# Input products of a gated recurrence in 512- and 256-column matmuls, two operands in other slots, and eight modulation blocks moved to the output projection

## The chip, the core and the metric

The kernel runs on one core of a Trainium2 chip. The metric is the device time of one execution in microseconds (us); each version is run several times and the median is taken. The engines are called as the profile calls them: PE (TensorE) multiplies, PEld loads its weights, DVE (VectorE) and ACT (ScalarE) work elementwise, SP issues the DMAs.

## The reference

One layer of a hybrid block on 256 tokens of width 2048, in f32. Every projection below is a dense product.

```python
mod = silu(c) @ ada_w + ada_b                    # six vectors of 2048: sh1, sc1, g1, sh2, sc2, g2
h = rmsnorm(x, norm1_g) * (1 + sc1) + sh1
z = h @ w_in                                     # split into q, kc, vc, ks, vs, kw, vw, g_nsa, lx, ly, ga, gb
o_a = nsa_attention(q, kc, vc, ks, vs, kw, vw, g_nsa, ...)   # 16 heads, 4 groups: compressed, selected, window branch
u = causal_dwconv(lx, conv_w, conv_b)            # 4 taps
r = sigmoid(blocks(u) @ w_a + b_a)               # 16 blocks of 128 x 128
i = sigmoid(blocks(u) @ w_i + b_i)
log_a = 8 * r * log_sigmoid(lam)
# scan over the tokens: s[t] = exp(log_a) * s[t-1] + sqrt(-expm1(2 * log_a)) * i * u
o_b = gelu(ly) * s
merged = sigmoid(ga) * (o_a @ proj_a) + sigmoid(gb) * (o_b @ proj_b)
x = x + g1 * (merged @ w_out)
h = rmsnorm(x, norm2_g) * (1 + sc2) + sh2
gate, val = split(h @ ffn_up)                    # 2 x 6144
x = x + g2 * ((gelu(causal_dwconv(gate)) * val) @ ffn_down)
return rmsnorm(x, final_g)
```

## The kernel before

Every dense product is done in three parts so that it keeps f32 accuracy in a faster format: weights W and activations X are each split into a rounded part and a rest, and the kernel sums X_hi W_hi, X_lo W_hi and X_hi W_lo. An activation tile `h1[:, kt, :]` therefore has 512 columns: 256 tokens of hi and, behind them, the same 256 tokens of lo.

Weights come in pieces of 1 MB, 128 x 2048. `stage` (L97) issues the DMA on SP's queue into one of four `raw` buffers. `split` (L102) turns each half of it into a `hi` tile (copy on ACT, L107) and a `lo` tile (subtraction on DVE, L108), three buffers of each. A split is issued at a raised priority. A piece in feature layout holds two output tiles of 128 features for eight k tiles.

Two helpers multiply such a piece. `dense_pair1` (L172) puts both output tiles into one bank, 256 columns each, and issues three 256-column products per weight tile: hi with X_hi, hi with X_lo, lo with X_hi (L185, L187, L188). `dense_pair` (L114) gives each output tile a bank of its own and issues two products per weight tile: hi with all 512 columns and lo with 256 (L130). Its bank holds two halves that have still to be added, and its products are kept in the order in which they are written (`keep_in_program_order`). `dense_tok` (L192) is the form with tokens on the partitions, for the gates, `w_proj`, `w_out` and `w_down`; all its products are 512 columns wide.

The stages in order of time are these. First the norm, the modulation and the projections for keys, values and queries. Then the attention and the input products of the recurrence (287 to 476 us): eight products `pr` of 32 weight tiles each into `lx` (L714 to L720), between them the attention units (g, t) of `attention` (L632), each with four heads of scores, softmax, transposes and the product `oT` (L693, L697). Then the recurrence (476 to 585 us): four tiles `bt` of 512 channels, each with the causal convolution on DVE (L740, L743), the gate products `lru_r` and `lru_i` on PE (L745, L747), sigmoids, tanh, exp and sqrt on ACT (L751 to L757), three 1024-wide steps and four scans on DVE (L758 to L762), and two products of the gelu branch (L765) with gelu (L767), product with the scan (L768) and split into `oB` (L771, L772). Then the merge (585 to 893 us), the output projection with `w_out` (893 to 984 us) and the FFN.

The modulation vectors g1, sc2, sh2 and g2 are 64 blocks of 128 numbers. Each is one 1 MB piece, multiplied by a row and summed in one 2048-wide pass on DVE (L234), followed by an addition of one column (L235). `filler(n)` issues the next n of these blocks where it is called: two behind each product of the lx loop (L720), two behind the gelu products with pr 0 and 4 (L773), two or four behind each `w_proj` product (L797).

The order of the instructions on each engine is not written out by hand. A scheduler sets it from dependencies, priorities and the point at which pools free their buffers. It keeps the loads on SP's queue, the activations that share a table (`tbl`) and the products of `dense_pair` in the order of the code. Tiles with the same tag share one slot: C0 to C7 hold, one after the other, `kvc`, the gathered keys of the compression (`gath`), the softmax results `pT`, `lx` (C4 to C7) and `oB`. `cmpb` holds the compressed values `vcmp` and the compressed probabilities in C7, and the first head's `p` of each attention unit lies in C3.

## Time and profile before

| what | value |
|---|---|
| runs | 1793.19, 1794.15, 1797.32 us (median 1794.15) |
| profiled execution | 1793.77 us, its span 1792.0 us |
| mean granted clock of PE | 0.997 of full speed |
| PE busy | 1771.6 us, 99% of the span, 10262 products |
| DVE busy | 1350.5 us, 75% |
| ACT busy | 881.9 us, 49% |
| DMA | 429.50 MB, mean 240 GB/s |

The busy shares are means over stages, so the windows by stage are read next to them. Matmuls are pipelined: a 256-column product is shown 0.28 us long, although the next one starts 0.12 us behind it. What a product costs PE is therefore read from the distance of the starts. A value in square brackets behind a row is the idle time of the engine before it, and the work that ended this idle time.

### The profile page before, as it was taken

The numbers are of one execution on the slowest core, as the hardware profiler recorded it, in microseconds if no ns is written. First come the engines' busy times: TensorE is split into PE (matmuls) and PEld (weight loads), VectorE is DVE, ScalarE is ACT, GpSimd is POOL, SyncE is SP. The second block draws the span as 40 slices with busy tenths as digits, with TensorE's granted clock in tenths as the row PEclk, the third lists the DMA queues.
The fourth block names the chain that finished last, engine by engine and source line by source line (L and its number), as shares of the span: only waits on it lengthen the run. The fifth ranks groups of instructions, "written<-read, shape, count | busy, mean of one in ns | idle before, by whom it ended". The sixth has DMA issues, their size and how long they took to land.

```text
span 1792.0 us, 25746 instructions
## 1 busy us (share of the span) xinstructions
PE 1771.6 (99%) x10262; PEld 1545.9 (86%) x10262; DVE 1350.5 (75%) x1976; ACT 881.9 (49%) x1202; POOL 0.2 (0%) x4
## 2 busy tenths in 40 slices
PE   8999999999999999999999999999999999999997
PEld 7999898888999888888888998888888888888886
DVE  7998897998698766767765997888555677766555
ACT  5644464655578444444445644444433444444443
POOL 0000000000000000000000000000000000000000
PEclk9999999999999999999999999999999999999999
DMA  9999864665646867777775566777655555555552
GB/s 350 379 335 355 288 245 161 235 212 203 221 173 227 303 237 290 286 292 281 294 266 195 186 235 235 282 282 282 239 193 200 191 188 188 188 188 188 190 198 106
DMA packets 64200, 429.50 MB, mean 240 GB/s; under 512 B 7088, under 2 KB 7376, under 8 KB 15568
## 3 DMA queue, kind: packets, MB, share of 16 engines
q1 hardware_dynamic: 63792, 427.08, 66.2%
q8 instruction: 80, 1.31, 0.3%
q10 hardware_dynamic: 288, 0.79, 0.1%
q14 instruction: 40, 0.33, 0.1%
HBM read 425.72 MB, written 2.11 MB: 239 GB/s over the span
## 4 chain that ended last, share of the span: by engine, by line
PE 86%; DVE 6%; DMA 4%; issue 2%; ACT 2%; SPq 0%; DVEq 0%; ACTq 0%
PE P L130 26%; PE P L204 12%; PE P L205 12%; PE P L203 12%; PE P L187 3%; PE P L188 3%; PE P L185 3%; DMA raw<-ada_w 2%; DVE lo L108 2%; PE P L464 2%; PE P L466 2%; PE P L465 2%; PE P L149 1%; PE P L148 1%; PE P L150 1%
## 5 line engine op out<-in xcount | busy, mean ns | idle before, releaser
L107 ACT ACTIVATE hi<-raw 128x1024 fp32r<-128x1024 f32 x588 | 622.0, 1060 | 764.5 <-PE P L205 325.5
L108 DVE TENSOR_TENSOR lo<-raw,hi 128x1024 fp32r<-128x1024 f32 x588 | 717.1, 1222 | 370.5 <-ACT hi L107 369.7
L130 PE MATMUL P<-h,hi 128*128 128x512 f32 x1344 | 463.9, 394 | 0.0
L130 PE MATMUL P<-h,lo 128*128 128x256 f32 x1344 | 366.4, 278 | 0.0
L130 PEld LDWEIGHTS P<-h,hi 128*128 128x128 f32 x1344 | 249.1, 188 | 54.9
L130 PEld LDWEIGHTS P<-h,lo 128*128 128x128 f32 x1344 | 252.4, 188 | 4.2
L234 DVE SCALAR_TENSOR_TENSOR raw<-raw,crow 128x2048 f32<-128x2048 f32 x64 | 146.2, 2285 | 3.6 <-DMA raw<-ada_w 3.2
L188 PE MATMUL P<-h,lo 128*128 128x256 f32 x512 | 147.6, 289 | 0.8 <-DVE lo L108 0.8
L187 PE MATMUL P<-h,hi 128*128 128x256 f32 x512 | 146.7, 287 | 0.0
L185 PE MATMUL P<-h,hi 128*128 128x256 f32 x512 | 146.7, 287 | 0.0
L464 PE MATMUL P<-h,hi 128*128 128x256 f32 x384 | 107.9, 285 | 0.3 <-ACT hi L107 0.3
L465 PE MATMUL P<-h,hi 128*128 128x256 f32 x384 | 107.6, 284 | 0.0
L466 PE MATMUL P<-h,lo 128*128 128x256 f32 x384 | 102.2, 284 | 0.0
L188 PEld LDWEIGHTS P<-h,lo 128*128 128x128 f32 x512 | 97.8, 191 | 1.8 <-DVE lo L108 1.4
L187 PEld LDWEIGHTS P<-h,hi 128*128 128x128 f32 x512 | 97.9, 191 | 1.4 <-issue 1.2
L185 PEld LDWEIGHTS P<-h,hi 128*128 128x128 f32 x512 | 97.9, 191 | 1.0 <-issue 0.7
L204 PE MATMUL P<-lo,ua 128*128 128x512 f32 x240 | 93.5, 390 | 0.3 <-DVE lo L108 0.3
L205 PE MATMUL P<-hi,ua 128*128 128x512 f32 x240 | 93.4, 389 | 0.0
L203 PE MATMUL P<-hi,ua 128*128 128x512 f32 x240 | 83.6, 389 | 0.0
L204 PE MATMUL P<-lo,h 128*128 128x512 f32 x192 | 75.5, 393 | 0.0
L464 PEld LDWEIGHTS P<-h,hi 128*128 128x128 f32 x384 | 74.0, 193 | 1.1 <-ACT hi L107 0.5
L205 PE MATMUL P<-hi,h 128*128 128x512 f32 x192 | 74.9, 390 | 0.0
(281 smaller groups left out, 3131.6 us busy)
## 6 DMA issues: line engine op xcount, KB each, us to landing
raw<-ada_w SPq DMA_DIRECT2D x96, 1024.0 KB, 5.0
raw<-w_up SPq DMA_DIRECT2D x96, 1024.0 KB, 4.8
raw<-w_down SPq DMA_DIRECT2D x48, 1024.0 KB, 4.9
raw<-w_lru SPq DMA_DIRECT2D x32, 1024.0 KB, 4.9
raw<-w_proj SPq DMA_DIRECT2D x32, 1024.0 KB, 5.1
raw<-w_gates SPq DMA_DIRECT2D x24, 1024.0 KB, 6.5
raw<-w_out SPq DMA_DIRECT2D x16, 1024.0 KB, 4.9
raw<-w_kv SPq DMA_DIRECT2D x24, 512.0 KB, 6.7
```

The costliest lines, as they stand in the source:

```text
L107: A.activation(hi[:, :n], raw[:, lo_col:lo_col + n], AF.Copy)
L108: V.tensor_tensor(lo[:, :n], raw[:, lo_col:lo_col + n], hi[:, :n].bitcast(F32), op=ALU.subtract)
L130: PE.matmul(ps[f][:, 0:256] if w else ps[f], hl[w][:, k * 256 + f * 128:k * 256 + f * 128 + 128], r[:, 0:256] if w else r, start=(kt == 0 ...
L185: PE.matmul(o, hi[:, sl], r[:, 0:256], start=(kt == 0 and f == 0), stop=False, skip_group_check=True)
L187: PE.matmul(o, hi[:, sl], r[:, 256:512], start=False, stop=False, skip_group_check=True)
L188: PE.matmul(o, lo[:, sl], r[:, 0:256], start=False, stop=(kt == n - 1), skip_group_check=True)
L203: PE.matmul(ps[j], xh, hi[:, w], start=(kt == 0), stop=False, skip_group_check=True)
L204: PE.matmul(ps[j], xh, lo[:, w], start=False, stop=False, skip_group_check=True)
L205: PE.matmul(ps[j], xl, hi[:, w], start=False, stop=(kt == n - 1), skip_group_check=True)
L234: V.scalar_tensor_tensor(raw, raw, 1.0, row, op0=ALU.mult, op1=ALU.mult, accum_out=modc[:, c:c + 1])
L464: PE.matmul(o, hi[:, sl], h1[:, kt, 0:256], start=first and f % 2 == 0, stop=False, skip_group_check=True)
L465: PE.matmul(o, hi[:, sl], h1[:, kt, 256:512], start=False, stop=False, skip_group_check=True)
```

## The change

The eight input products of the recurrence go through `dense_pair` without the fixed order, so each weight tile has one 512- and one 256-column product. `add_halves` adds the two halves: per output tile ACT copies the second half out of the bank and DVE adds the first half. The gelu branch keeps `dense_pair1`. `cmpb` moves to C3, `gat` to C7 and `gath` to C2, C4, C5 and C6; the first head's `p` goes into the small slot "xp". The softmax's short steps on DVE (clamp, reciprocal, product with the gates) are done once for two heads, and two heads' transposes follow together. The lx loop issues one modulation block per product where it issued two; in the merge the blocks are spread over the pieces of a product; eight blocks go between the pieces of the first three quarters of `w_out`. The shift columns of `hp` are written behind that loop. `w2t` and `hs`, and the two `gp` tiles of a gate pair in the FFN, share one tile each.

```diff
-        def dense_pair(pieces, rhs):
+        def dense_pair(pieces, rhs, pinned=True):
...
-                    for w in (0, 0, 1, 0, 1, 0, 1, 1) + (0, 1) * 4 if ip + half == 0 else (0, 1) * 8:
+                    for w in (0, 0, 1, 0, 1, 0, 1, 1) + (0, 1) * 4 if pinned and ip + half == 0 else (0, 1) * 8:
...
-                        tc.keep_in_program_order(
-                            PE.matmul(ps[f][:, 0:256] if w else ps[f], hl[w][:, k * 256 + f * 128:k * 256 + f * 128 + 128],
...
+                        mm = PE.matmul(ps[f][:, 0:256] if w else ps[f],
+                                       hl[w][:, k * 256 + f * 128:k * 256 + f * 128 + 128], r[:, 0:256] if w else r,
+                                       start=(kt == 0 and not w), stop=(kt == n - 1 and w == 1), skip_group_check=True)
+                        if pinned:
+                            tc.keep_in_program_order(mm)
             return ps
+
+        def add_halves(dst, p):
+            A.activation(dst, p[:, 256:512], AF.Copy)
+            with tc.high_priority(200):
+                V.tensor_tensor(dst, p[:, 0:256], dst, op=ALU.add)
...
-        def dense_tok(pieces, lhs, late=None):
+        def dense_tok(pieces, lhs, late=None, fills=()):
...
+                if ip in fills:
+                    filler()
...
-        cmpb = big.tile([128, 1024], F32R, tag="C7", name="cmpb")
+        cmpb = big.tile([128, 1024], F32R, tag="C3", name="cmpb")
...
-                g = big.tile([128, 16, 4, NCMP], F32, tag="C6", name="gat")
+                g = big.tile([128, 16, 4, NCMP], F32, tag="C7", name="gat")
...
-                    q = big.tile([128, 8, 2, 60], F32R, tag="C%d" % (2 + 2 * a + n), name="gath")
+                    q = big.tile([128, 8, 2, 60], F32R, tag="C%d" % (2, 4, 5, 6)[2 * a + n], name="gath")
...
-                if hh == 0:
-                    p = big.tile([128, 512], F32, tag="C3", name="p")
-                else:
-                    p = tmp.tile([128, 512], F32, tag=("r", "iu", "tt")[hh - 1], bufs=1, name="p")
...
+                p = tmp.tile([128, 512], F32, tag=("xp", "r", "iu", "tt")[hh], bufs=1, name="p")
...
+                heads.append(p)
+                if hh % 2 == 0:
+                    continue
+                w = sm[:, 1, hh - 1:hh + 1]
+                V.tensor_scalar(w, w, 1e-30, None, op0=ALU.max)
+                V.reciprocal(w, w)
+                V.tensor_tensor(w, w, gates[:, hh - 1:hh + 1, 1:3], op=ALU.mult)
+                turn_heads(hh - 1)
+                turn_heads(hh)
...
         for pr in range(8):
-            pl = dense_pair1([w_lru[pr, k] for k in range(2)], h1r)
-            A.activation(lx[pr // 2][:, 2 * (pr % 2):2 * (pr % 2) + 2],
-                         pl.rearrange("p (f t) -> p f t", f=2), AF.Copy)
+            ps = dense_pair([w_lru[pr, k] for k in range(2)], h1r, False)
+            for f in range(2):
+                add_halves(lx[pr // 2][:, 2 * (pr % 2) + f], ps[f])
             if units:
                 attention(*units.pop(0))
-            filler(2)
+            filler()
...
-                    ps = dense_tok([w_gates[n - 1, s, k] for k in range(4)], h1r)
+                    ps = dense_tok([w_gates[n - 1, s, k] for k in range(4)], h1r, fills=(1, 3))
...
-                ps = dense_tok([w_proj[n, s, k] for k in range(4)], rhs)
+                ps = dense_tok([w_proj[n, s, k] for k in range(4)], rhs, fills=(1, 3))
...
-                filler(2 if n == 0 else 4)
...
-            ps = dense_tok([w_out[n, k] for k in range(4)], lambda kt: mg[kt // 2][:, kt % 2])
+            ps = dense_tok([w_out[n, k] for k in range(4)], lambda kt: mg[kt // 2][:, kt % 2],
+                           fills=(0, 1, 3) if n < 2 else (0, 2) if n == 2 else ())
```

The scheduler now orders several stretches in another way. The first place is PE's order at the end of the attention. In the rows before, the last product of the lx loop (P_5013) ends, then come the last gate products of tile 1 of the recurrence (`lru_i`), then the first product of the gelu branch (P_5196).

```order
L185 MATMUL P_5013<-h1_169,hi_5102 128x256
L187 MATMUL P_5013<-h1_169,hi_5102 128x256
L188 MATMUL P_5013<-h1_169,lo_5103 128x256
L747 MATMUL lru_i_5146<-lt_5139,raw_5143 128x256 x2
L747 MATMUL lru_i_5160<-lt_5139,raw_5143 128x256 x2
L185 MATMUL P_5196<-h1_169,hi_5199 128x256
L187 MATMUL P_5196<-h1_169,hi_5199 128x256
L188 MATMUL P_5196<-h1_169,lo_5200 128x256
L185 MATMUL P_5196<-h1_169,hi_5199 128x256
```

After the change the last gate products of tile 1 (lru_i_4831) stand inside the third product of the gelu branch (P_5174), and the gate products of tile 2 (lru_r_5123, lru_i_5124) right behind them; the last attention product oT_4315 stands within the second gelu product, 23 rows further up.

```order
L191 MATMUL P_5174<-h1_169,hi_5177 128x256
L193 MATMUL P_5174<-h1_169,hi_5177 128x256
L194 MATMUL P_5174<-h1_169,lo_5178 128x256
L191 MATMUL P_5174<-h1_169,hi_5177 128x256
L193 MATMUL P_5174<-h1_169,hi_5177 128x256
L765 MATMUL lru_i_4831<-lt_4810,raw_4814 128x256 x2
L763 MATMUL lru_r_5123<-lt_5119,raw_5121 128x256
L765 MATMUL lru_i_5124<-lt_5119,raw_5121 128x256
L763 MATMUL lru_r_5123<-lt_5119,raw_5121 128x256
L765 MATMUL lru_i_5124<-lt_5119,raw_5121 128x256
L194 MATMUL P_5174<-h1_169,lo_5178 128x256
L191 MATMUL P_5174<-h1_169,hi_5177 128x256
```

Two and a bit of the eight gelu products have moved ahead of the end of tile 1's gate products, and tile 2's have moved up to them.

The second place is ACT's order at the same point, the activations of tile 1 (`lt` tiles, L751 to L757 before, L769 to L775 after; an `ACT_TABLE_LOAD` stands where the next function lies in another table). Before, the tanh, exp and sqrt stand between the copies `hi` of three pieces:

```order
L107 ACTIVATE hi_5329<-raw_5327 128x1024
L755 ACTIVATE lt_5142<-lt_5140 128x512
L756 ACT_TABLE_LOAD
L756 ACTIVATE lt_5140<-lt_5140 128x1024
L757 ACT_TABLE_LOAD
L757 ACTIVATE lt_5142<-lt_5142 128x1024
L107 ACTIVATE hi_5357<-raw_5327 128x1024
L107 ACTIVATE hi_5387<-raw_5385 128x1024
L767 ACT_TABLE_LOAD
L767 ACTIVATE lt_5139<-P_5196 128x512
L107 ACTIVATE hi_5415<-raw_5385 128x1024
L107 ACTIVATE hi_5506<-raw_5504 128x1024
```

After the change, the exp and the sqrt, two gelus and the sigmoids of tile 2 stand in one run ahead of hi_5263. The copy before it, hi_5235, stands six rows above the first row shown; three sigmoids, a tanh and a table load are between.

```order
L774 ACTIVATE lt_4811<-lt_4811 128x1024
L775 ACT_TABLE_LOAD
L775 ACTIVATE lt_4813<-lt_4813 128x1024
L785 ACT_TABLE_LOAD
L785 ACTIVATE lt_4810<-P_4867 128x512
L785 ACTIVATE lt_4810<-P_4997 128x512
L769 ACT_TABLE_LOAD
L769 ACTIVATE lt_5119<-lru_r_5123,cols_113 128x256
L770 ACTIVATE lt_5120<-lru_i_5124,cols_113 128x256
L769 ACTIVATE lt_5119<-lru_r_5123,cols_113 128x256
L770 ACTIVATE lt_5120<-lru_i_5124,cols_113 128x256
L107 ACTIVATE hi_5263<-raw_5233 128x1024
```

From one copy to the next there were at most five instructions here, and now there are 16, four of them table loads.

The third place is DVE's order for the same tile: the three 1024-wide steps, the scans, and the gelu branch's first product (L758 to L768 before, L776 to L786 after).

```order
L758 TENSOR_TENSOR lt_5141<-lt_5141,lt_5139 128x1024
L108 TENSOR_TENSOR lo_5330<-raw_5327,hi_5329 128x1024
L759 SCALAR_TENSOR_TENSOR lt_5142<-lt_5140,lt_5142 128x1024
L108 TENSOR_TENSOR lo_5358<-raw_5327,hi_5357 128x1024
L760 TENSOR_TENSOR lt_5142<-lt_5142,lt_5141 128x1024
L108 TENSOR_TENSOR lo_5388<-raw_5385,hi_5387 128x1024
L762 SCALAR_TENSOR_TENSOR lt_5141<-lt_5140,lt_5142 128x256 x4
L108 TENSOR_TENSOR lo_5416<-raw_5385,hi_5415 128x1024
L768 TENSOR_TENSOR lt_5139<-lt_5139,lt_5141 128x512
L108 TENSOR_TENSOR lo_5507<-raw_5504,hi_5506 128x1024
L772 TENSOR_TENSOR oB_5315<-lt_5139,oB_5315 128x2x256
L108 TENSOR_TENSOR lo_5535<-raw_5504,hi_5534 128x1024
```

After the change:

```order
L776 TENSOR_TENSOR lt_4812<-lt_4812,lt_4810 128x1024
L777 SCALAR_TENSOR_TENSOR lt_4813<-lt_4811,lt_4813 128x1024
L778 TENSOR_TENSOR lt_4813<-lt_4813,lt_4812 128x1024
L771 TENSOR_SCALAR lt_5119<-lt_5119,lsm4_90 128x256 x2
L780 SCALAR_TENSOR_TENSOR lt_4812<-lt_4811,lt_4813 128x256 x4
L108 TENSOR_TENSOR lo_5264<-raw_5233,hi_5263 128x1024
L786 TENSOR_TENSOR lt_4810<-lt_4810,lt_4812 128x512
L771 TENSOR_SCALAR lt_5119<-lt_5119,lsm4_90 128x256
L786 TENSOR_TENSOR lt_4810<-lt_4810,lt_4812 128x512
L771 TENSOR_SCALAR lt_5119<-lt_5119,lsm4_90 128x256
L776 TENSOR_TENSOR lt_5120<-lt_5120,lt_5119 128x1024
L108 TENSOR_TENSOR lo_5300<-raw_5297,hi_5299 128x1024
```

Before, a `lo` stood between any two steps of the tile; now lo_5264 stands behind the whole run with the scans, and the first steps of tile 2 (L771, L776) are among those that follow.

## Rows read from the trace of the kernel before

**Rows 1.** Page part 1: busy us, share of the span, instructions.

```profile
PE 1771.6 (99%) x10262; PEld 1545.9 (86%) x10262; DVE 1350.5 (75%) x1976; ACT 881.9 (49%) x1202; POOL 0.2 (0%) x4
```

**Rows 2.** Windows by stage, all engines.

```profile
core 0: us, PE busy (x) PEld busy (x) DVE busy (x) ACT busy (x) POOL busy (x), PEclk, DMA share, GB/s
287.00:476.00 189.00, 188.50 (x1297) 159.59 (x1296) 164.33 (x445) 109.78 (x266) 0.00 (x0) 1.00 0.56 199
476.00:585.00 109.00, 108.18 (x854) 106.10 (x853) 92.72 (x133) 84.79 (x111) 0.00 (x0) 1.00 0.59 212
893.00:984.00 91.00, 91.00 (x418) 75.20 (x418) 56.11 (x70) 45.37 (x63) 0.00 (x0) 1.00 0.66 239
```

**Rows 3.** Timeline of PE, recurrence: start, length, engine, line, tiles; 35 rows between.

```profile
500.20 0.28 PE L185 MATMUL P<-h,hi 128*128 128x256 f32 x1
...
504.52 0.28 PE L185 MATMUL P<-h,hi 128*128 128x256 f32 x1
```

**Rows 4.** Timeline of PE, FFN, where pairs run; 33 rows between.

```profile
1200.46 0.39 PE L130 MATMUL P<-h,hi 128*128 128x512 f32 x1
...
1206.36 0.40 PE L130 MATMUL P<-h,hi 128*128 128x512 f32 x1
```

**Rows 5.** Timeline of PE, three holes between 287 and 585 us.

```profile
329.14 0.55 PE L689 MATMUL tp<-cols,p 128*128 128x128 f32 x3 [0.50 <-ACT pcT L661]
516.91 0.39 PE L188 MATMUL P<-h,lo 128*128 128x256 f32 x1 [0.17 <-DVE lo L108]
551.78 0.28 PE L187 MATMUL P<-h,hi 128*128 128x256 f32 x1
552.71 0.38 PE L188 MATMUL P<-h,lo 128*128 128x256 f32 x1 [0.65 <-DVE lo L108]
```

**Rows 6.** Timeline of ACT, start of the recurrence.

```profile
486.14 0.47 ACT L751 ACTIVATE lt<-lru_r,cols 128x256 f32<-128x256 f32 x1
486.49 0.48 ACT L752 ACTIVATE lt<-lru_i,cols 128x256 f32<-128x256 f32 x1
487.83 0.61 ACT L755 ACTIVATE lt<-lt 128x512 f32<-128x512 f32 x1
488.47 1.28 ACT L756 ACT_TABLE_LOAD   x1
489.76 1.06 ACT L756 ACTIVATE lt<-lt 128x1024 f32<-128x1024 f32 x1
492.12 1.06 ACT L757 ACTIVATE lt<-lt 128x1024 f32<-128x1024 f32 x1
493.09 1.99 ACT L107 ACTIVATE hi<-raw 128x1024 fp32r<-128x1024 f32 x2
496.39 0.60 ACT L767 ACTIVATE lt<-P 128x512 f32<-128x512 f32 x1
```

**Rows 7.** The chain that ended last: start, length, engine, tile.

```profile
465.44 1.73 PE lru_r L745 x8
```

**Rows 8.** Timeline of DVE, recurrence.

```profile
483.10 0.35 DVE L753 TENSOR_SCALAR lt<-lt,lsm 128x256 f32<-128x256 f32 x1
497.76 2.43 DVE L762 TENSOR_TENSOR_SCAN lt<-lt 128x256 f32<-128x256 f32 x4
500.11 1.20 DVE L108 TENSOR_TENSOR lo<-raw,hi 128x1024 fp32r<-128x1024 f32 x1
501.23 0.68 DVE L768 TENSOR_TENSOR lt<-lt 128x512 f32<-128x512 f32 x1
510.71 0.74 DVE L740 TENSOR_SCALAR lt<-lx,cols 128x256 f32<-128x256 f32 x2
514.46 1.26 DVE L743 SCALAR_TENSOR_TENSOR lt<-lx,cols,lt 128x253 f32<-128x253 f32 x3
531.55 2.29 DVE L234 SCALAR_TENSOR_TENSOR raw<-raw,crow 128x2048 f32<-128x2048 f32 x1 [0.15 <-DMA raw<-ada_w]
```

**Rows 9.** Page part 6: DMA issues, KB each, us from issue to landing.

```profile
raw<-w_out SPq DMA_DIRECT2D x16, 1024.0 KB, 4.9
```

More of the change, by code (lines that the diff above doesn't have):

```diff
@@ L413, in compress @@
                 return
-            hs = tmp.tile([128, 4, 64], F32, tag="xp", bufs=2, name="hs")
+            hs = wh[:, 1].rearrange("p (g n) -> p g n", g=4)
             V.memset(hs, 0.0)
@@ L664, in attention, with turn_heads @@
             nj = 2 * (t + 1)
+            sm = tmp.tile([128, 2, 4, 2], F32, tag="sm", bufs=2, name="sm")
+            heads = []
+            def turn_heads(hh):
+                p = heads[hh]
+                for b in range(2):
+                    pb = p[:, b * nk:b * nk + nk]
+                    V.tensor_scalar(pb, pb, sm[:, 1, hh, b:b + 1], None, op0=ALU.mult)
+                tp = psx.tile([128, 512], F32, tag="t", bufs=1, name="tp")
+                for j in range(nj):
+                    PE.transpose(tp[:, j * 128:j * 128 + 128], p[:, j * 128:j * 128 + 128], ident)
+                for n in range(t + 1):
+                    A.activation(pT[n][:, :, hh, :], tp[:, n * 256:n * 256 + 256].rearrange("p (j q) -> p j q", q=128),
+                                 AF.Copy)
             for hh in range(4):
@@ L684, in attention @@
-                for b in range(2):
-                    pb = p[:, b * nk:b * nk + nk]
-                    V.tensor_scalar(pb, pb, sm[:, 4 + b:5 + b], None, op0=ALU.mult)
-                tp = psx.tile([128, 512], F32, tag="t", bufs=1, name="tp")
-                for j in range(nj):
-                    PE.transpose(tp[:, j * 128:j * 128 + 128], p[:, j * 128:j * 128 + 128], ident)
-                for n in range(t + 1):
-                    A.activation(pT[n][:, :, hh, :], tp[:, n * 256:n * 256 + 256].rearrange("p (j q) -> p j q", q=128),
-                                 AF.Copy)
+                p = tmp.tile([128, 512], F32, tag=("xp", "r", "iu", "tt")[hh], bufs=1, name="p")
@@ L822, in block_kernel @@
         sdev = small["sdev"]
-        for n in range(8):
-            sh = modc[:, 48 + 2 * n:50 + 2 * n].unsqueeze(2).to_broadcast([128, 2, 2])
-            A.activation(hp[n][:, :, 0, 256:258], sh, AF.Copy)
-            V.tensor_tensor(hp[n][:, :, 1, 256:258], sh, hp[n][:, :, 0, 256:258].bitcast(F32), op=ALU.subtract)
         def add_rows(ps, j, n, row):
@@ L855, in block_kernel @@
                 tc.keep_in_program_order(A.activation(warm, col("eps"), AF.Sqrt))
+        for n in range(8):
+            sh = modc[:, 48 + 2 * n:50 + 2 * n].unsqueeze(2).to_broadcast([128, 2, 2])
+            A.activation(hp[n][:, :, 0, 256:258], sh, AF.Copy)
+            V.tensor_tensor(hp[n][:, :, 1, 256:258], sh, hp[n][:, :, 0, 256:258].bitcast(F32), op=ALU.subtract)
         rstd(sdev, sums)
-        dr = tmp.tile([128, 2, 128], F32, tag="xp", bufs=2, name="dr")
+        dr = tmp.tile([128, 2, 128], F32, tag="xp", bufs=1, name="dr")
         for j in range(2):
@@ L881, in block_kernel @@
                     b = half * 24 + gr * 2 + f
[L882 removed]
+                    gps = tmp.tile([128, 2, 256], F32, tag="xp", bufs=1, name="gp") if f == 0 else gps
+                    gp = gps[:, f]
                     take(gp, f)
```

20 lines of the change are left out of this document (7 added, 13 removed).

## The prediction, made before the changed kernel was run

> **What bounds the kernel now.** First the page's busy shares: PE is busy 99% of the span of 1792.0 us [rows 1]. Busy PE is not PE at its peak, so next the windows by stage, where the granted clock stands at its upper level, 2.4 GHz, throughout [rows 2], and then the distances between the starts of matmuls. The stage with the attention and the input products of the recurrence (287 to 476 us) has DVE busy 164.33 of 189 us and ACT 109.78; the recurrence itself (476 to 585 us) has ACT busy 84.79 and DVE 92.72 of 109 us; in the output projection (893 to 984 us) DVE has 56.11 of 91 us [rows 2]. In a quiet stretch of the recurrence the starts of 128x256 products stand at a fixed distance: 12 triples in 4.32 us, 0.360 us a triple, 0.120 us each [rows 3]. In the FFN the pair of one 512-column and one 256-column product is as regular: 17 pairs in 5.90 us, 0.347 us a pair [rows 4]. PE therefore issues without holes nearly everywhere. In 287 to 585 us I find three holes worth naming [rows 5]: 329.14 (a transpose waits 0.50 us for ACT's pcT), 516.91 and 552.71 (a product waits 0.17 and 0.65 us for DVE's lo). Between the starts 551.78 and 552.71 lie 0.93 us instead of 0.12, so 0.81 us are lost, 0.16 more than the row's idle time; the other two lose 0.66 and 0.33 by the same addition. So PE is the bound, the time can fall only through fewer or shorter issue slots or through these holes, and each new hole is lost for good.
>
> **The change, part by part.** The sum is made against the profiled execution, 1793.8 us, 0.4 below the median of three runs.
>
> *Columns.* Eight input products of 32 weight tiles each, 256 triples, become 256 pairs of the kind that the FFN runs: 256 x (0.360 - 0.347) = **-3.2 us**, to be had only where PE issues without holes. At the same 768 columns three products take 13 ns more than two. The Trainium skill, TensorE: Matmul & The Clock Gate, section Back-to-back issue gap, gives N/2.4 + 2.5 ns for a full-clock product: an estimate from it is 328 ns for the triple and 325 for the pair, a gain of 0.7 us in all. The rows on both forms in this very kernel say otherwise, and the rule returns below as a rival.
>
> *Evictions.* Per product two 256-wide copies on ACT and two adds on DVE replace one 512-wide copy. No row has this shape out of a product's bank; the bounds are nothing and the 512-wide rows, 0.60 us on ACT [rows 6] and 0.68 on DVE [rows 8]. Both engines have slack there [rows 2], and eight modulation blocks of 2.29 us [rows 8] leave DVE in that stage, while 48 short softmax instructions go too. I take 0 for this. The hole at 329 us hangs on an attention chain with more slack now: **-0.66** (bounds -0.66 to +1).
>
> *Where the attention ends.* This is the edit that I think decides. The order of PE shows that with half of the modulation blocks gone the scheduler packs the input products more densely and the attention units further apart. Before, the gate products of tile 1 of the recurrence stand directly ahead of the first gelu product; now two and a bit of the eight gelu products stand ahead of them, and those of tile 2 stand right behind. The recurrence is no longer spread out. On ACT, 16 instructions now stand between hi_5235 and hi_5263, four of them table loads; with the prices below that run takes 11.3 us. Before, the run with the table loads was five instructions long (tanh, load, exp, load, sqrt) and took 5.3 us, from 487.83 to 493.09, and the three hi buffers covered it without a hole [rows 6]. On DVE lo_5264 now stands behind the scan of tile 1, where before a lo stood between any two steps.
>
> *First hole.* Count from the end of the last attention product oT_4315. ACT, by the lengths in [rows 6] less the 0.1 by which neighbours other than loads overlap there (sigmoids start 0.35 apart): oA 0.5, taken like a gelu of the same 512 columns; load 1.28; three sigmoids 1.08; tanh 0.53; sigmoid 0.36; hi_5235 1.0; three sigmoids 1.08; tanh 0.53; load 1.28; exp 1.07; load 1.28; sqrt 0.97; load 1.28; two gelus 1.0; load 1.28; three sigmoids 1.08: 15.6 us. Then DVE [rows 8]: two short multiplies 0.5, four scans 2.35, lo_5264 1.2: 4.1. So lo_5264 is there after 19.7 us. PE in the same time has 94 products at 0.120 and 12 gate matmuls; each of these stands twice in the trace, and eight records take 1.73 us [rows 7], so 0.43 each; 16.4 us. PE therefore waits 3.3 us with no time for the hand-overs between engines; with an estimated 0.5 us for five of them, **+3.8**. Bounds: 0, if the lead of the buffers is larger than the order lets me see, and 4.3. Behind lo_5264 on DVE stand the end of tile 1 and every later lo; behind PE's product the rest of the gelu branch.
>
> *After it.* PE has no lead left. From lo_5264 to lo_5786 the order gives PE 312 products and 8 gate products, 40.9 us. DVE has 13 splits at 1.13 (14.7), five other 1024-wide steps (5.7), two modulation blocks at 2.21 (4.4), four scans (2.35), eight 512-wide steps at 0.60 (4.8), 28 steps of the causal convolution at 0.39 and 0.33 (10.5) and six short multiplies at 0.27 (1.6): 44.1 us, each by its length in [rows 8] less the 0.08 by which neighbours overlap there. Without a single wait on DVE that is 3.3 us more than PE has; with its waits for the sqrt of tile 2 (ACT's loads again) and PE's for one late hi I come to 7.0. I take **+4.5**, nearer to the lower bound. The two holes of before in this stage go into this: **-1.1**.
>
> *Modulation blocks moved.* Eight blocks, each one 1 MB DMA on SP's queue, one 2048-wide pass on DVE and a short add, go into the first three quarters of the output projection: 8 x 2.3 = 18 us of DVE, which then has 74 of 91 us there. What they could hold up are the weight pieces behind them on SP, which wait for one of four raw buffers; a piece lands in 4.9 us [rows 9], PE needs 5.5 for its 24 products of 512 columns (0.23 each: the pair's 0.347 less 0.12) and at most one block stands between two pieces. In the merge before it the blocks are only spread between pieces. I count 0 (bounds 0 and +9: four of eight blocks each holding PE for their 2.3 us). The shift columns of hp written after that loop are short and in ACT's and DVE's order stand among the splits: 0.
>
> *Operand slots* change when tiles come free, not the work: 0; vcmp and the first p no longer sit where lx and the gathered keys go, which removes waits that no row shows.
>
> Sum: 1793.8 - 3.2 - 0.7 - 1.1 + 3.8 + 4.5 = **1797.1 us**, a slowdown of 0.18%.
>
> **The rivals.**
> *The recurrence keeps up.* Then only the first terms are left: 1793.8 - 3.2 - 0.7 - 1.1 = 1788.8, faster. It decides if ACT and DVE need no more than PE's 16.4 us from oT_4315 to lo_5264, that is if 3.3 us of the chain fall away. For it: before, a run of 5.3 us was covered without a hole [rows 6]. Against: this one is twice as long, and three buffers hold 3 x 2.88 us of products (24 at 0.120 each).
> *First hole only.* DVE's surplus is absorbed because PE's hole lets DVE run ahead: 1793.8 - 5.0 + 3.8 = 1792.6, the same. For it: DVE in 476 to 585 us has 16 us idle [rows 2]. Against: that idle time lies in another place of the order.
> *The columns give nothing.* Products between f32 attention matmuls may not reach the FFN's distance: at a gain of 0.7 us the sum is 1799.6. That is what the rule of the skill would give; the traces so far show 0.360 and 0.347 and bear it out badly.
> *The output projection stalls too.* Its four raw buffers now carry seven pieces a quarter; at +5 to +9 the time is 1802 to 1806.
>
> **How the numbers follow.** No measurement of this kernel can tell less than about 0.2% (3.6 us) from no change. The forecast, 1794.5 to 1801 by its own bounds, gets 0.55, of which 0.33 lies above 1797.7 and 0.22 below; the recurrence that keeps up 0.17, of which 0.15 are beyond 0.2%; the first hole alone 0.14; columns without gain 0.04; the projection 0.10. Slower 0.33 + 0.04 + 0.08 = 0.45, same 0.22 + 0.14 + 0.02 + 0.02 = 0.40, faster 0.15. The range 1789 to 1803 leaves out a part of the fastest case and of the slowest.
>
> **What would show it.** Products in pairs at 0.347 us in the input products of the recurrence (L129); PE idle for about 4 us, released by DVE's lo, some 16 us after the last oT, with four table loads on ACT in that time; further holes of 0.3 to 1.5 us, same releaser, in the 40 us behind; no idle PE in the output projection, DVE near 80% there. If the lo rows of that place come before PE asks for them, the third step is wrong and the time falls to 1789.

## The result and the profile after

The changed kernel takes 1807.51 us (median of 4 runs, 1807.3 to 1808.79), the kernel before 1795.49 us in the same count. The recorded ratio is 1.0075 with a 95% interval of 1.0063 to 1.0088, a little above the quotient of these two medians (1.0067): slower, by about four times what was forecast, and above the stated range. The profiled execution took 1807.71 us, 13.9 more than that of before; its span is 1805.7 us.

The page's busy shares of the changed kernel, which answer to [rows 1]:

```profile
PE 1774.8 (98%) x10006; PEld 1536.5 (85%) x10006; DVE 1353.4 (75%) x1944; ACT 889.1 (49%) x1214; POOL 0.2 (0%) x4
```

PE has 256 products less, as the pairs want it, and is idle 31 us instead of 20. The windows by stage (columns as in [rows 2]; the first four rows are the attention with the input products, the recurrence, the merge and the output projection, the last three are short stretches behind holes):

```profile
288.00:503.00 215.00, 213.17 (x1245) 171.65 (x1245) 160.83 (x402) 124.02 (x288) 0.00 (x0) 0.99 0.47 164
503.00:597.00 94.00, 86.35 (x650) 83.35 (x649) 78.66 (x117) 76.48 (x100) 0.00 (x0) 0.98 0.51 184
597.00:907.50 310.50, 308.20 (x1371) 254.46 (x1371) 220.96 (x242) 132.38 (x145) 0.00 (x0) 1.00 0.78 288
907.50:998.00 90.50, 90.50 (x416) 74.86 (x415) 70.42 (x92) 45.56 (x66) 0.00 (x0) 1.00 0.80 306
...
331.80:335.30 3.50, 3.50 (x12) 3.01 (x13) 3.23 (x9) 2.78 (x4) 0.00 (x0) 0.53 0.72 281
523.50:526.30 2.80, 2.80 (x15) 2.80 (x15) 2.80 (x6) 2.59 (x4) 0.00 (x0) 0.50 0.77 234
599.90:603.00 3.10, 3.10 (x14) 2.56 (x15) 3.10 (x4) 1.41 (x3) 0.00 (x0) 1.00 0.88 330
```

Attention and recurrence together went from 298 to 309 us. The attention's last product starts at 501.7 us instead of 474.2, so its stage is 26 us longer, and the recurrence, squeezed, has 94 us instead of 109. The output projection keeps its time with DVE at 70.42 of 90.50 us. The timeline of PE shows the holes, and at 394 us two starts of 512-column products with seven more pairs between them:

```profile
330.20 0.66 PE L685 MATMUL tp<-cols,p 128*128 128x128 f32 x4 [1.09 <-ACT pcT L671]
331.23 0.49 PE L711 MATMUL oT<-pcT,cmpb 47*128 47x512 f32 x1 [0.37 <-DVE oA L720]
338.92 0.70 PE L692 MATMUL s<-kT,qT 128*128 128x256 f32 x2 [0.37 <-ACT p L700]
...
394.27 0.39 PE L129 MATMUL P<-h,hi 128*128 128x512 f32 x1
...
397.05 0.40 PE L129 MATMUL P<-h,hi 128*128 128x512 f32 x1
...
520.59 0.38 PE L191 MATMUL P<-h,hi 128*128 128x256 f32 x1 [2.14 <-ACT hi L107]
523.13 0.58 PE L194 MATMUL P<-h,lo 128*128 128x256 f32 x1 [2.04 <-DVE lo L108]
557.24 0.39 PE L194 MATMUL P<-h,lo 128*128 128x256 f32 x1 [0.88 <-DVE lo L108]
567.73 0.38 PE L191 MATMUL P<-h,hi 128*128 128x256 f32 x1 [1.60 <-ACT hi L107]
599.88 0.50 PE L211 MATMUL P<-lo,oA 128*128 128x512 f32 x1 [2.30 <-DVE lo L108]
```

From the one start of 394.27 us to the other at 397.05 eight pairs take 2.78 us, 0.347 each, as in [rows 4]. The two holes at 518 to 523 us are the forecast first hole, which comes in two parts: PE waits for hi_5263 and, a few products on, for lo_5264. By the distance of the starts they lose 2.30 and 2.20 us. Later holes of 0.34 to 1.04 us wait for `lo`, as forecast; the largest, 1.76 us ahead of 567.73, waits for a copy `hi` on ACT. What stood on ACT meanwhile, of its timeline the two copies, the four loads and the sqrt of tile 1:

```profile
506.35 1.04 ACT L107 ACTIVATE hi<-raw 128x1024 fp32r<-128x1024 f32 x1
...
509.60 1.28 ACT L774 ACT_TABLE_LOAD   x1
511.96 1.28 ACT L775 ACT_TABLE_LOAD   x1
513.25 1.06 ACT L775 ACTIVATE lt<-lt 128x1024 f32<-128x1024 f32 x1
514.33 1.28 ACT L785 ACT_TABLE_LOAD   x1
516.73 1.28 ACT L769 ACT_TABLE_LOAD   x1
519.47 1.07 ACT L107 ACTIVATE hi<-raw 128x1024 fp32r<-128x1024 f32 x1
```

Between the two copies lie the 16 instructions with four table loads, from 507.3 to 519.5 us, 12.2 us; the forecast had 11.3 us for them (11.2 by its own prices). And DVE's timeline, at the same place and at the start of the merge:

```profile
514.34 1.23 DVE L777 SCALAR_TENSOR_TENSOR lt<-lt 128x1024 f32<-128x1024 f32 x1 [4.29 <-ACT lt L775]
519.53 2.43 DVE L780 TENSOR_TENSOR_SCAN lt<-lt 128x256 f32<-128x256 f32 x4
521.88 1.20 DVE L108 TENSOR_TENSOR lo<-raw,hi 128x1024 fp32r<-128x1024 f32 x1
...
593.46 2.43 DVE L780 TENSOR_TENSOR_SCAN lt<-lt 128x256 f32<-128x256 f32 x4
595.81 2.27 DVE L243 SCALAR_TENSOR_TENSOR raw<-raw,crow 128x2048 f32<-128x2048 f32 x1
598.60 1.22 DVE L108 TENSOR_TENSOR lo<-raw,hi 128x1024 fp32r<-128x1024 f32 x1
```

lo_5264 ends 20.8 us after ACT took up the last attention product (502.28 us); the forecast had 19.7. PE's own work in that time is about 16.5 us (from 502.1 to 523.1 us, less 4.5 of holes); the forecast had 16.4. At 595.81 a modulation block of the merge stands between the last scans and the first split that the merge waits for: the idle time of 2.30 us at 599.88, which the forecast did not have.

Where the input products stand against the attention is read from PE's timeline: the last of their 512 products starts at 471.60 us, 30 us ahead of the last attention product, and the row behind it, at 471.80, is of the gelu branch (L191).

```profile
471.60 0.36 PE L129 MATMUL P<-h,lo 128*128 128x256 f32 x1
```

### The profile page after: what moved, and what is told of

The parts are those of the page before. It is cut to its first block, busy times and chain, and to the rows that moved or that the text cites. A ratio compares the mean times of both kernels' runs of the same rounds, so it can differ in the third digit from the quotient of the medians.

```text
span 1805.7 us, 25201 instructions
## 1 busy us (share of the span) xinstructions
PE 1774.8 (98%) x10006; PEld 1536.5 (85%) x10006; DVE 1353.4 (75%) x1944; ACT 889.1 (49%) x1214; POOL 0.2 (0%) x4
## 4 chain that ended last, share of the span: by engine, by line
PE 91%; DVE 4%; ACT 3%; issue 1%; DMA 1%; DVEq 0%; SPq 0%; ACTq 0%
PE P L129 31%; PE P L211 12%; PE P L212 12%; PE P L210 12%; PE P L474 2%; PE P L475 2%; PE P L476 2%; PE P L155 1%; PE P L154 1%; DVE lo L108 1%; PE P L156 1%; PE P L468 1%; PE P L469 1%; PE P L467 1%; PE s L692 1%
## 5 line engine op out<-in xcount | busy, mean ns | idle before, releaser
L129 PE MATMUL P<-h,hi 128*128 128x512 f32 x1600 | 558.7, 396 | 0.0
L129 PEld LDWEIGHTS P<-h,hi 128*128 128x128 f32 x1600 | 297.9, 188 | 65.4 <-issue 0.7
L129 PEld LDWEIGHTS P<-h,lo 128*128 128x128 f32 x1600 | 301.4, 188 | 5.0 <-issue 0.7
L243 DVE SCALAR_TENSOR_TENSOR raw<-raw,crow 128x2048 f32<-128x2048 f32 x64 | 146.5, 2289 | 33.7 <-DMA raw<-ada_w 33.5
L474 PE MATMUL P<-h,hi 128*128 128x256 f32 x384 | 107.9, 285 | 0.0
L475 PE MATMUL P<-h,hi 128*128 128x256 f32 x384 | 107.8, 285 | 0.0
L191 PE MATMUL P<-h,hi 128*128 128x256 f32 x256 | 73.3, 287 | 3.7 <-ACT hi L107 3.7
L474 PEld LDWEIGHTS P<-h,hi 128*128 128x128 f32 x384 | 74.1, 193 | 0.3 <-issue 0.2
L475 PEld LDWEIGHTS P<-h,hi 128*128 128x128 f32 x384 | 74.2, 193 | 0.0
L193 PE MATMUL P<-h,hi 128*128 128x256 f32 x256 | 73.9, 289 | 0.0
L332 DVE SCALAR_TENSOR_TENSOR raw<-raw,crow 128x2048 f32<-128x2048 f32 x31 | 70.8, 2286 | 0.9 <-DMA raw<-ada_w 0.7
L476 PEld LDWEIGHTS P<-h,lo 128*128 128x128 f32 x384 | 70.6, 192 | 0.3 <-issue 0.2
```

The costliest lines, as they stand in the source:

```text
L129: mm = PE.matmul(ps[f][:, 0:256] if w else ps[f], hl[w][:, k * 256 + f * 128:k * 256 + f * 128 + 128], r[:, 0:256] if w else r, start=(kt ...
L193: PE.matmul(o, hi[:, sl], r[:, 256:512], start=False, stop=False, skip_group_check=True)
L243: V.scalar_tensor_tensor(raw, raw, 1.0, row, op0=ALU.mult, op1=ALU.mult, accum_out=modc[:, c:c + 1])
L474: PE.matmul(o, hi[:, sl], h1[:, kt, 0:256], start=first and f % 2 == 0, stop=False, skip_group_check=True)
L475: PE.matmul(o, hi[:, sl], h1[:, kt, 256:512], start=False, stop=False, skip_group_check=True)
L476: PE.matmul(o, lo[:, sl], h1[:, kt, 0:256], start=False, stop=last, skip_group_check=True)
```

## The experiments

Each run is compared with the kernel before on the same chip; the ratio has its 95% interval. "Hole" is time lost between two starts of products, beyond their usual distance; "half clock" is a stretch in which the profile shows a granted clock of 0.50. Holes and windows are those of one profiled execution each.

| run | what it is | median us | ratio to before |
|---|---|---|---|
| e1 | before, pairs alone | 1801.07 | 1.0035 [1.0023, 1.0048] |
| e2 | changed, compression's slots back | 1812.81 | 1.0100 [1.0086, 1.0114] |
| e3 | changed, merge's blocks back | 1809.47 | 1.0082 [1.0069, 1.0096] |
| e4 | changed, eight blocks back to the lx loop | 1808.44 | 1.0079 [1.0065, 1.0093] |
| e5 | changed, triples | 1800.77 | 1.0037 [1.0024, 1.0051] |
| e6 | changed, paced | 1802.24 | 1.0046 [1.0034, 1.0059] |
| e7 | before, pairs, paced | 1798.49 | 1.0031 [1.0018, 1.0043] |
| e8 | changed, softmax by head | 1804.28 | 1.0058 [1.0044, 1.0072] |
| e9 | before, pairs, paced more loosely | 1796.27 | 1.0012 [1.0003, 1.0021] |
| e10 | before, triples in two banks | 1793.85 | 0.9998 [0.9989, 1.0007] |
| e11 | before, operand slots alone | 1794.79 | 1.0001 [0.9992, 1.0011] |
| e12 | before, pairs, second piece paced | 1793.23 | 0.9998 [0.9989, 1.0007] |
| e13 | before, moved blocks alone | 1797.27 | 1.0021 [1.0012, 1.0030] |

**e1, the pairs alone.** Of the change only this, with its helpers:

```diff
-            pl = dense_pair1([w_lru[pr, k] for k in range(2)], h1r)
...
+            ps = dense_pair([w_lru[pr, k] for k in range(2)], h1r, False)
+            for f in range(2):
+                add_halves(lx[pr // 2][:, 2 * (pr % 2) + f], ps[f])
```

> The kernel before with the input products of the recurrence in 512- and 256-column products and nothing else changed. Theory A (the columns pay what the rows of before promise, and the recurrence is squeezed only where the columns meet the other operand slots): in its order of ACT no run between two copies hi is as long as the 16 instructions with four table loads of the changed kernel; the longest in the recurrence have 6 instructions with three loads, 6.3 us by the row lengths, so no hole over 1.5 us in the recurrence, and 1790 to 1793 us, 2 to 4 below before. Theory B (two banks for each product, out of four, are enough to squeeze the recurrence): holes of 2 us and more at the first gates, and at or above the time of before, 1796 to 1803 us.

It came as theory B has it in time and holes, 6.8 us above before; theory B's cause, the two banks, is tested in e10. PE's timeline:

```profile
471.23 0.66 PE L695 MATMUL tp<-cols,p 128*128 128x128 f32 x4 [0.72 <-ACT pcT L667]
472.64 0.66 PE L695 MATMUL tp<-cols,p 128*128 128x128 f32 x4 [0.75 <-ACT pT L697]
474.97 2.08 PE L751 MATMUL lru_r<-lt,raw 128*128 128x256 f32 x4 [1.68 <-ACT p L685]
478.45 1.09 PE L695 MATMUL tp<-cols,p 128*128 128x128 f32 x4 [0.68 <-DVE p L692]
525.22 0.38 PE L194 MATMUL P<-h,lo 128*128 128x256 f32 x1 [2.03 <-DVE lo L108]
```

In the last attention units PE has no products left to put between transposes and scores, and waits for the softmax itself: 5.8 us in 467 to 478 us. From the gates at 475 us to 483.8 us the granted clock stands at 0.50. The last input product starts 24 us ahead of the last attention product (466.5 and 491.0 us).

**e2, the slots.** `cmpb` back to C7, `gat` to C6, `gath` to C2 to C5.

```diff
-        cmpb = big.tile([128, 1024], F32R, tag="C3", name="cmpb")
+        cmpb = big.tile([128, 1024], F32R, tag="C7", name="cmpb")
...
```

> The changed kernel with cmpb, gat and gath in their slots of before (C7, C6, C2 to C5); wide products, paired softmax and the moved blocks stay. Theory A (the slots let the last two input products run ahead of the last attention units, and so squeeze the gates): the two holes of 2.3 and 2.2 us at 518 to 521 us, the half-clock stretch behind them and most of the later holes fall away, 8 to 10 us; 1797 to 1800 us. Theory B (slots only change when tiles come free): within 2 us of the changed kernel's 1807.5.

Neither: 5.3 us slower than the changed kernel by the medians, 4.5 by the ratios. `cmpb` lies in C7 until the attention ends, and the last quarter of lx wants C7. PE's timeline:

```profile
476.82 1.13 PE L763 MATMUL lru_r<-lt,raw 128*128 128x256 f32 x4 [1.70 <-ACT p L700]
482.61 0.58 PE L191 MATMUL P<-h,hi 128*128 128x256 f32 x1 [1.55 <-DVE lx L139]
531.80 0.58 PE L191 MATMUL P<-h,hi 128*128 128x256 f32 x1 [4.91 <-ACT hi L107]
```

A product waits for the lx eviction (L139), and the hole at the gates is 5.1 us instead of 4.5. With the pairs the new slots help; that the squeeze comes from them, theory A, is refuted.

**e3, the merge's blocks.** 

```diff
...
-                ps = dense_tok([w_proj[n, s, k] for k in range(4)], rhs, fills=(1, 3))
+                ps = dense_tok([w_proj[n, s, k] for k in range(4)], rhs)
...
                 m.append(sg)
+                filler(2 if n == 0 else 4)
```

> The changed kernel with the modulation blocks of the merge behind each product, as before; its order is the changed kernel's up to the merge. Theory A (the 2.5 us hole at 597 us is the modulation block that now stands between the last scans and the first splits of the merge): this hole goes and nothing else moves, 1804.5 to 1805.5 us. Theory B (DVE is late there from the recurrence anyway, the block only fills the wait): the hole stays at 1.5 us or more, 1807 us.

At the merge theory A holds: the block no longer stands ahead of the first split, and the hole falls from 2.47 to 0.49 us. But the time does not fall: the output projection takes 4.2 us more (95.0 instead of 90.9), 2.2 of them in holes that the changed kernel does not have (the first at 926.98) and most of the rest behind them, where the granted clock stands at 0.50 from 929.6 to 933.0 us. PE:

```profile
595.23 0.50 PE L211 MATMUL P<-lo,oA 128*128 128x512 f32 x1 [0.33 <-DVE lo L108]
...
926.98 0.73 PE L210 MATMUL P<-hi,mg 128*128 128x512 f32 x2 [0.68 <-ACT hi L107]
```

ACT, where the releaser is a weight piece that came late:

```profile
925.87 2.01 ACT L107 ACTIVATE hi<-raw 128x1024 fp32r<-128x1024 f32 x2 [4.13 <-DMA raw<-w_out]
```

**e4, the blocks of the lx loop.**

```diff
-            filler()
+            filler(2)
...
-                           fills=(0, 1, 3) if n < 2 else (0, 2) if n == 2 else ())
```

> The changed kernel with two modulation blocks per input product again and none in the output projection. Theory P, the prediction's own (the recurrence is squeezed because half of the blocks left the input products): the holes at 518 to 521 us go, 8 to 10 us less, 1798 to 1800 us. Theory A (columns and slots squeeze it, the blocks have no part): the same run of 16 instructions with four loads on ACT, the same two holes, and a time within 2 us of the changed kernel's 1807.5.

Theory A: the same two holes (2.54 and 2.20 us) and the same time. The prediction's own theory P had 1798 to 1800 us. The prediction's cause for the squeeze is refuted.

**e5, triples.** The reverse of e1's diff, on the changed kernel.

> The changed kernel with the input products of the recurrence as three 256-column products again, all else as changed. Theory A2, after the first four runs (with the pairs PE's order puts the input products ahead of the attention: an attention unit then takes about 25 us of PE's order instead of 20, the input products are used up two units before the end, and the last units and the first gates stand bare): with the triples the units are 20 us apart again, the first two holes and the half-clock stretch behind them go (6 us), later ones shrink by 2 or 3, the columns' 2 to 3 us are lost, the holes at 328 to 338 us and the one at the start of the merge stay: 1800 to 1803 us. Theory C (slots, softmax and blocks squeeze it by themselves): 1807 to 1810 us.

As theory A2 expects, 6.7 us below the changed kernel. The last attention product comes at 472.3 us instead of 501.7, and the holes of the recurrence sum to 1.6 us instead of 8.5.

**e6 and e7, paced.** One order edge on PE, on the changed kernel and on e1:

```diff
         for pr in range(8):
+            with ExitStack() as behind:
+                if pr:
+                    behind.enter_context(tc.issue_after(steps[pr].ins))
-            ps = dense_pair([w_lru[pr, k] for k in range(2)], h1r, False)
+                ps = dense_pair([w_lru[pr, k] for k in range(2)], h1r, False)
```

`steps[n]` is the last transpose of attention unit n.

> The changed kernel, same instructions, with one order edge on PE: input product n (n from 1) stands behind the last transpose of attention unit n, so that the products are not used up early. By its order the units are 19.5 us apart and the gates stand as before. Theory A2: the holes at 518 to 521 us, the half-clock stretch and most later ones go, 7 to 9 us; the holes at 328 to 338 us and at the merge stay: 1798 to 1801 us. Theory D (ACT and DVE have too much work for these stages in any order): holes of the same sum appear in the attention instead, where PE waits for a unit's transposes before it may go on with products: 1805 to 1810 us.

> The kernel before with the pairs for the input products and the same order edge, nothing else. Theory A2: the holes of the run with the columns alone at 467 to 480 us (6 us), its half-clock stretch (2 us) and the hole at 523 us (2 us) go; the columns pay 2 to 3 us: 1790 to 1793 us, below before. Theory D: 1798 to 1803 us.

Half of each theory. The holes of the recurrence sum to 1.1 us in both runs, the attention ends at 476.9 us in e6, and the median is 5.3 and 2.6 us lower than without the edge; the second difference is not clear of noise, as the intervals of e1 and e7 overlap for the most part. The last input product now starts 8 us behind the last attention product (484.5 and 482.8 us). But between 360 and 470 us PE now waits in the attention, mostly ahead of transposes, 5.8 us in e6 and 5.5 in e7.

**e8, softmax by head.** The softmax of one head after the other, as before:

```diff
-                if hh % 2 == 0:
-                    continue
...
-                turn_heads(hh - 1)
-                turn_heads(hh)
```

> The changed kernel with the softmax of the attention head by head, as before. By its order ACT has four table loads around the sigmoids of the merge gates at 320 to 330 us where the changed kernel has six, and in the recurrence a longest run of 8 instructions with three loads, 7.4 us, instead of 16 with four, 11.1 us. Theory E (the pairing of heads makes the holes at 328 to 338 us, 2.3 us, with 1.5 us at half clock behind them): these go; the recurrence keeps holes of about half the size: 1800 to 1804 us. Theory F (the pairing has no part; the 48 short steps come back on DVE): 1807 to 1810 us.

3.2 us below the changed kernel, and theory E holds for the attention: in the windows PE is busy from the first scores to the recurrence without a hole, at the upper clock.

```profile
286.80:510.00 223.20, 223.20 (x1332) 182.02 (x1331) 170.70 (x456) 132.39 (x301) 0.00 (x0) 1.00 0.46 166
```

The holes of the recurrence don't halve, against what was expected: they grow from 8.5 to 11.7 us, in nine of 0.6 to 2.2 us, while the one at the start of the merge falls from 2.5 to 0.7 us. So the 3.2 us are a balance of stages and not the price of the attention's holes alone.

What pairing the heads does on ACT shows in the changed kernel's rows: four table loads between 320 and 328 us, and behind them pcT, for which the transposes of 330.20 wait.

```profile
320.49 1.28 ACT L810 ACT_TABLE_LOAD   x1
322.42 1.28 ACT L700 ACT_TABLE_LOAD   x1
324.75 1.28 ACT L810 ACT_TABLE_LOAD   x1
326.69 1.28 ACT L657 ACT_TABLE_LOAD   x1
329.57 0.58 ACT L671 ACTIVATE pcT<-tpc 47x512 fp32r<-47x512 f32 x1
```

From 317 to 337 us every profile with paired heads has six loads (the changed kernel and e2 to e6), and every one without has four (before, e1, e7 to e13).

**e9, paced more loosely.** The edge of e7 behind the third head's transposes instead of the fourth's:

```diff
-                if hh == 3:
+                if hh == 2:
                     steps.append(last_tp)
```

> The kernel before with the pairs and the order edge of the seventh run, but behind the transposes of the third head of attention unit n instead of the last head's; in PE's order the units then stand about where they stand before (141, 160, 182 us of PE time after the first scores, before 141, 160, 182). Theory A2 (what the pairs cost is only the lost cover of the attention): the waits of PE for transposes at 381 to 467 us of the seventh run, 5.5 us, shrink to 2 us or less, the columns pay 2 us: 1791.5 to 1795 us, at or just below before. Theory D (the attention's chain has about 20 us a unit and needs that cover in any order, and the pairs only take cover away): 3 us or more of such waits stay, wherever the edge stands: 1796 to 1799 us.

```profile
381.07 0.66 PE L695 MATMUL tp<-cols,p 128*128 128x128 f32 x4 [0.89 <-ACT pT L699]
464.33 0.66 PE L695 MATMUL tp<-cols,p 128*128 128x128 f32 x4 [0.82 <-ACT pT L699]
```

The waits stay, 5.0 us, as theory D says. But the rows (PE's timeline) name the releaser: the copy pT that empties the one bank of the transposes. The edge itself lets two heads' transposes follow each other without a product between.

**e12, second piece paced.** So here only the second weight piece of a product is held back; the condition stands inside the helper:

```diff
+                        elif after is not None and 2 * ip + half >= 2:
+                            tc.add_manual_dep(mm.ins, after.ins.name, NOSYNC, reason="behind the unit")
```

> The kernel before with the pairs; only the second weight piece of input product n is held behind the last transposes of attention unit n, the first piece is free. In PE's order no two heads' transposes are neighbours any more, the units end at 106, 125, 145, 164 and 185 us (before 98, 120, 141, 160 and 182) and the gates of the recurrence stand within 3 us of before. Theory G (the waits of the two paced runs came from neighbouring transposes, which share one bank): waits in the attention under 2 us, recurrence as before, the columns pay 2 to 3 us: 1790.5 to 1793.5 us, below before. Theory D (the chain of the attention needs the cover that the pairs took away): 3 us or more of waits in 360 to 480 us again, or in the first gates: 1795 to 1799 us.

Theory G for the waits: 1.7 us of them up to 480 us; one hole over 0.3 us is left at the gates:

```profile
515.80 0.39 PE L196 MATMUL P<-h,lo 128*128 128x256 f32 x1 [1.03 <-DVE lo L108]
```

Not for the time: the median, 1793.23 us, lies in theory G's range, but the ratio of 0.9998 with an interval over 1 does not put it below before. From the first scores to the merge it has 297.5 us, before 297.9, in one execution each. Most of the pairs' gain goes into what is left of waits. No version that beats both kernels came out of this.

**e10 and e11, controls.** e10 gives each output tile of a triple product its own bank, e11 takes the slots alone.

```diff
-            p = bank()
+            ps = [bank(), bank()]
...
-                        o = p[:, f * 256:f * 256 + 256]
+                        o = ps[f][:, 0:256]
```

> The kernel before with triples, but each output tile of an input product in a bank of its own (256 of its 512 columns used), so two of four banks for a product, and two 256-wide evictions on ACT. If the two banks squeeze the schedule, the order of PE and the time go the way of the run with the columns alone, 1799 to 1803 us; if it is the width of the pairs, by which the order is made, the order stays that of before, as its rows show, and the time too: 1793 to 1796 us.

> The kernel before with cmpb, gat, gath, the first head's p and the small tiles in the slots of the changed kernel, nothing else. By its order every engine has the order of before in the attention and the recurrence. Theory: slots cost and give nothing without the pairs, 1793 to 1796 us. Rival: tiles that share xp, one buffer instead of two, make the FFN's gate pairs wait: 1796 us or more, with idle PE behind 1000 us.

Both are the time of before. Two banks alone don't squeeze anything, and slots cost nothing without pairs. e10 evicts each bank with a copy and has no addition at raised priority; the pairs have one, and no run tells its part from that of the products' width.

**e13, the moved blocks alone.** The `fills` and `filler` lines of the change on the kernel before, as:

```diff
-            filler(2)
+            filler()
...
+                           fills=(0, 1, 3) if n < 2 else (0, 2) if n == 2 else ())
```

> The kernel before with the moved modulation blocks alone (one per input product, spread in the merge, eight in the output projection, shift columns behind it), triples, slots of before for the compression and softmax by head; only p of head 0 and the small tiles lie in xp. By its order the longest run on ACT in the recurrence has 6 instructions with three loads, 6.3 us. Theory A2 (the blocks have no part in the squeeze, but one of them stands between the last splits of the recurrence and the first of the merge): no hole over 1 us up to 585 us, one of about 2 us at the start of the merge, nothing in the output projection: 1795 to 1797 us. The prediction's theory (the squeeze comes from the blocks): holes of 3 us and more in the recurrence, 1798 us or more.

3.3 us above before, just above what theory A2 expects, and none of the 3 us holes of the prediction's theory. No hole over 0.9 us up to 585 us, and one of 1.86 us at the start of the merge:

```profile
589.54 0.50 PE L211 MATMUL P<-lo,oA 128*128 128x512 f32 x1 [1.70 <-DVE lo L108]
```

A block ahead of this split does not always cost so much: in e2, e6 and e8 one stands there too, but behind a `lo` that follows the scans, and the hole is 0.7 us.

## Why the prediction was wrong

The direction was right, and so was the mechanism of the two terms that made the forecast, the holes of the recurrence; what brings these holes about was not, and terms of about 8 us were missing or had the wrong sign. The terms against the profile after, summed on the 1793.8 us of before:

| term of the sum | forecast us | measured us |
|---|---|---|
| columns | -3.2 | -2.2 |
| hole at 329 us, attention | -0.7 | +1.7, and +1.5 at half clock |
| old holes of the recurrence | -1.1 | -1.1 |
| first hole | +3.8 | +4.5, and +1.5 at half clock |
| after it | +4.5 | +4.0 |
| modulation blocks: merge | 0 | +2.5 |
| modulation blocks: output projection | 0 | 0 |
| ahead of the first scores | none | +1.0 |
| sum | 1797.1 | 1807.2 |

The profiled execution took 1807.7; the other 0.5 us are not assigned to a row. The prediction calls 1794.5 to 1801 us the bounds of its forecast; its terms at their bounds, without the modulation blocks, add to 1792.1 to 1801.8. The measured time lies outside both.

**Columns: mis-sized.** In quiet stretches a triple costs 0.358 us (mean of the starts at 322 to 476 us of before) and a pair 0.349 (327 to 505 us of after): 8.7 ns by 256, not 13. An estimate by the formula of the Trainium skill, TensorE: Matmul & The Clock Gate, section Back-to-back issue gap, which the page gives for an isolated product, is a gain of 0.6 us in all (0.7 in the prediction, by rounding). The starts measured here, 232.9 ns for 512 columns and 116.6 for 256 in a pair, decide for 2.2.

**The steps that failed are three that stood at nothing or at a gain.** *Evictions* had the softmax's change as slack for the attention and -0.66 for the hole at 329 us. The hole grew instead, two others came, and 3.4 us of PE time at half clock behind them: 3.9 us off, the largest error. e8 takes back the pairing of heads alone and all of this is gone from the attention. With the pairing ACT has six table loads there where four were; that these loads make the hole is read from the rows, and no run changes them alone. *Modulation blocks moved* counted 0 for the merge because the blocks are only spread between pieces. One of them came to stand ahead of the first split, and e13 has that hole with nothing but the blocks. The output projection did as forecast, but e3 shows how near the danger was. *First hole* and *After it* met their sizes within 0.7 us, but without the clock: the prediction had no price for PE's slower products behind a hole, 1.5 us here. The first met it by its own working (PE 16.5 us against 16.4, the chain through DVE 20.8 against 20.2 with the hand-overs). The second was luck in part: it was picked between 3.3 and 7.0, and 1.8 of its 4.0 us wait for `hi` on ACT, while the signs named DVE's `lo`.

**Where the attention ends: right in what it read, wrong in its cause.** The order and the long run on ACT were as read. That half of the blocks being gone brings them about is refuted (e4, e13). The pairs with their eviction do (e1, e5), not their two banks (e10): with pairs the order sets the input products ahead of the attention; the units, by the starts of their last products, are 25.5 us apart on the mean in the changed kernel (323.4 to 501.7 us), 21.4 before, 21.6 with triples in e5. The products that would cover the last units and the first gates are then used up: the last one starts 30 us ahead of the last attention product in the changed kernel and 24 in e1, but 1 to 8 us behind it in e6, e7, e9 and e12, where the largest hole at the gates is 0.3 to 1.2 us (0.3 before). Why the scheduler sets them so is not settled: the order is fixed ahead of the run, and that it reckons the pairs shorter against the attention's steps than the chip does is only argued.

**Where the columns' gain went.** With the order mended (e7, e9, e12) waits of the attention take the place of the gain. PE's products are not only work: between transposes and scores they cover a chain on ACT and DVE; the units stand 21 us apart even where PE waits for it (e6, 20.6 to 21.5 from the third unit on). The chain is not always so long: in e5 two units take 18.9 us each and PE does not wait, so where the transposes stand has a part, as e9 and e12 show. That the cover is short even when spread well is argued from e12 alone: the time of before, with 0.5 us gained of 2.2 in one execution.

**Operand slots at 0** was right alone (e11), and wrong together with pairs (e2). The four parts' differences (pairs 6.8, blocks 3.3, slots 0.3 from before; softmax 3.2 back from the changed kernel) add to 13.6 us, and the ratio of 1.0075 is 13.5, though e2 shows that they are not independent, and e8 that its 3.2 us are a balance; that the sum fits is in part luck.

**The rivals.** The recurrence that keeps up and the first hole only are refuted by the rows after. The columns gave 2.2 us, between the 0.7 of the rival without gain and the forecast's 3.2. The projection that stalls did not come here, but in e3.

## What to carry to other kernels

An engine that is busy 99% can still be tied to a chain of others: before shortening its products, ask what they cover, and see in the order whether they still stand where the chain waits. When a scheduler remakes the order, a change of one product's form moves everything, so test each part alone, and read where the filler work runs out. A short block of other work costs nothing only where the split behind it has a lead.

## What the runs showed that was not expected

Two holes of 2.3 and 2.2 us within 5 us were followed by 3.4 us of products at 0.213 us instead of 0.120, granted clock 0.50, the lower level of 1.2 GHz; so were holes of 1.26 and 0.53 us at 328.7 to 331.2 us (0.53), and in e2 one hole of 5.1 us (0.50 from 531.8 to 536 us). One hole of 2.5 us at 597 us was not: the clock behind it stands at 1.00. The size of a hole does not settle it: in e4 the like hole of 2.5 us at the start of the merge was followed by 3.3 us at 0.50 (601.7 to 605 us), and behind the two holes of 2.3 and 2.2 us e3 has 6.1 us at 0.50 (520.7 to 526.8) where the changed kernel has 3.4. So a stretch costs 1.5 to 2.8 us more than its hole, and these 1.5 us of the changed kernel are one execution's.

The time ahead of the first scores, where the kernels do the same work, lies between 285.4 and 289.1 us in the 15 profiles; so 1.0 us of the difference between two profiled executions says nothing of the change.
